# RWKV's sample group: four pairs of heads together in the odd mixer's second part, in place of one pair at a time

## The chip, the cores and the metric

The kernel runs on one core of one Trainium2 chip. The metric is the device time of one execution in microseconds (us); a comparison uses the median of several executions of each kernel.

## The reference, cut to what matters

One inference step of a two-layer decoder for a prompt (512 positions) and a group of 8 samples of 4 positions that share all weights, 544 columns in all. Each layer is FFN, mixer, FFN. The odd layer's mixer projects its input once, runs a dilated windowed attention (8 heads) and an RWKV-7 recurrence (8 heads of 64) beside each other, and joins them in one output projection. The change concerns the recurrence of the 8 samples, which start from given states:

```
def step(s, inp):
    r_t, w_t, k_t, v_t, kk_t, a_t = inp
    sk = jnp.einsum('bhvk,bhk->bhv', s, kk_t)
    s = (s * w_t[:, :, None, :] - sk[..., None] * (kk_t * a_t)[:, :, None, :]
         + v_t[..., None] * k_t[:, :, None, :])
    return s, jnp.einsum('bhvk,bhk->bhv', s, r_t)
...
s_final, ys = lax.scan(step, s0.astype(f32), seq)
```

Outputs are the mixed result of all 544 columns and the final states of the samples (8 x 8 heads of 64 x 64) and of the prompt.

## The kernel before, in words

The kernel is written with tiles: each tile has a name, a pool and a number of buffers, and a planner that runs when the program is built simulates the engines and fixes the order of the instructions on each of them. Among instructions that it holds ready, the one that stands earlier in the program goes first; a tile of a pool with one buffer can be written again only when all readers of the one before are through. Every engine then works through its own list in order; a DMA is issued by the engine whose queue it is given to (SP for nearly all loads, ACT or POOL for some) and waits there for its buffer.

`odd_mix` (line 1670) does the odd mixer. It has two parts with different PSUM banks (a PSUM bank holds 128 x 512 floats; there are eight).

The first part has the kinds mm 2, ps 2, rs 2, rx 1, ro 1. RWKV's 8 heads are worked as four pairs p = 0 to 3; two pairs make a group. For each pair:

- `rw_first(p)` (line 1336 on) is a generator in three pieces: projections and decays; the chunks' products (line 1422) and a round trip through DRAM (rab, rEA); and then the forward substitution of 31 steps of two short VectorE operations each (lines 1440 and 1441), its table's way through DRAM (rtb, and line 1445 back into the tile TT), MT (line 1449), RR (line 1448), KB, VU and QB. Most of its tiles have one buffer, so a pair's later pieces wait for the pair before.
- `odd_qk(h)` (line 1129 on), the attention's query and key projections, is put between to fill TensorE.
- `rw_inverse(p)` (line 1482 on) is some 300 small products in banks of the kind rs (lines 1498, 1514, 1519, 1523, 1528); its last evictions are on line 1531.
- `rw_rec(g)` (line 1533) is the recurrence over 16 chunks for a group: 15 steps of a small product (line 1544) and a VectorE addition (line 1545), then the output products (line 1552) and `rw_out`. The group's tiles MT, W, RR and Y have one buffer, so pair 2's MT and RR wait for the recurrence of group 0.
- `rw_sample(p)` (line 1585) is the sample group of one pair. It loads the pair's states (S0, 128 x 512, on ACT's queue, line 1597), and then goes through a chain: products of the small vectors held in SM (lines 1605 to 1608), a masked copy, products (1615, 1616), a few sums, products (1622), products (1626, 1627), the product with the state (1633), a masked product and a sum over it on VectorE (1635, 1636), small additions (1638), the products for the output (1641), a masked product on GpSimd (1644), the update product (1647), decay of the state on GpSimd (1648), their sum (1649) and the store (1650). Its small matrices lie in the tile rsw, its masked products in rum; rS0, rsw and rum have one buffer each. The trace drops digits from names (rS is rS0).

In the program's order pair 0 has: pieces of rw_first, odd_qk(0), rw_inverse(0), rw_sample(0); pair 1 the same with rw_rec(0) ahead of rw_sample(1); pair 2 rw_inverse(2) and rw_sample(2); pair 3 odd_qk(2) and rw_inverse(3).

The second part has the kinds mm 1, sc 4, sm 1, rx 1, ro 1. It holds rw_rec(1), rw_sample(3) in banks of the kind sm, odd_qk(3), then 16 attention units `odd_head(hp, i)` (line 1141 on), each of which copies its queries on GpSimd into qz (line 1155), uses two banks sc for the scores (1156), two for the transposed weights (1169) and one for the values (1178), with adaLN's products (line 185) between the last eight units, and then `odd_sample` (line 1191), the attention of the sample group. `odd_sample` goes through `sample_attn` (line 500) twice, for four samples each: scores (516), softmax, transposes (539 to 541), values (549), output (561). Its cache tiles (4 x 256 KB a sample) are loaded on line 1204 into a ring of five places: the two halves of rKB, the two halves of rVU, and rGP0. `rw_sample_end` (line 1652) finishes the samples' output, and the output projection follows, whose first product is line 460 with the tile mm.

What the change touches in `odd_mix`, all of it:

```
                if p < 3:
                    self.rw_sample(p)
...
            self.psum(mm=1, sc=4, sm=1, rx=1, ro=1)
...
            self.rw_rec(1, r0, a2)
            self.rw_sample(3, "sm")
            for h in (3,):
                self.odd_qk(h, a1)
```

Of the kernel before, what the change touches and what calls it, by code (L numbers as in the profile page):

```python
# [9 lines left out]
F32 = mybir.dt.float32  # L10
# [16 lines left out]
class Kern:  # L27
# [1557 lines left out]
    def rw_sample(self, p, kind="rs"):  # L1585
# [4 lines left out]
        SM, DC = self.SM[:, p], self.DC  # L1590
# [4 lines left out]
        E = lambda n: self.rsm.tile([128, 512], F32, name=n)  # L1595
        S0 = E("rS0")
        nc.scalar.dma_start(bv(S0), D["rw_s0"][:, p])
        w = E("rsw")

        MS = w[:, 0:96].rearrange("p (a t) -> p a t", a=3)  # L1600
        EV, T, BK, QT, UV, W = [w[:, i:j] for i, j in ((96, 192), (192, 224), (224, 288), (288, 352), (352, 416), (416, 480))]
        pa = bank()
        pv = pa[:, 0:96].rearrange("p (a t) -> p a t", a=3)
        for o, r0, r1 in heads:
            PE.matmul(pv[o, 0], SM[o, 0:2], SM[o, 6])
            PE.matmul(pv[o, 1:3], SM[o, 6:8], SM[o, 0:4:3])
            PE.matmul(pa[o, 128:192], SM[o, 4:6], self.ident[o, o])
            PE.matmul(pa[o, 192:256], SM[o, 0:2], self.ident[o, o])
        V.tensor_tensor(MS, pv, self.rc["rsmask"][:, 0:3], op=M)
        S_.activation(UV, pa[:, 192:256], AF.Copy, scale=self.rc["rbmt"][:, 8:9])  # L1610
        S_.activation(w[:, 224:352], pa[:, 128:256], AF.Copy)

        pa = bank()
        for o, r0, r1 in heads:
            PE.matmul(pa[o, 0:32], MS[o, 0:2], MS[o, 1])
            PE.matmul(pa[o, 32:96], MS[o, 1:3], UV[o])
        S_.activation(EV, pa[:, 0:96], AF.Copy)
        V.tensor_tensor(T, self.rc["rsmask"][:, 3], MS[:, 1], op=S)
        V.tensor_tensor(T, T, EV[:, 0:32], op=A)
        pa = bank()  # L1620
        for o, r0, r1 in heads:
            PE.matmul(pa[o, 0:32], MS[r0, 0:2], EV[r0, 0:32])
        V.tensor_tensor(T, T, pa[:, 0:32], op=S)
        px = bank()
        for o, r0, r1 in heads:
            PE.matmul(px[o, 0:32], QT[r0], T[r0])
            PE.matmul(px[r0, 32:96], T[r0], EV[r0, 32:96])
        S_.activation(SM[:, 2], px[:, 0:32], AF.Copy)
        for o, r0, r1 in heads:
            V.tensor_copy(UV[r0], px[r0, 32:96])  # L1630
        pa = bank()
        for o, r0, r1 in heads:
            PE.matmul(pa[o], SM[o, 2:4], S0[o])
        um = bv(E("rum"))
        V.tensor_tensor(um, bv(pa), b8, op=M)
        V.tensor_reduce(W, um.rearrange("p b v -> p v b"), axis=AX.X, op=A)
        for o, r0, r1 in heads:
            V.tensor_tensor(UV[r0], UV[r0], W[r0], op=A)
        pa = bank()
        for o, r0, r1 in heads:  # L1640
            PE.matmul(pa[o, 0:64], MS[o, 1:3], UV[o])
        V.tensor_tensor(self.ys[:, p], W, pa[:, 0:64], op=A)

        G.tensor_tensor(um, UV.unsqueeze(1).to_broadcast([128, 8, 64]), b8, op=M)
        pa = bank()
        for o, r0, r1 in heads:
            PE.matmul(pa[o], BK[o], um[o].rearrange("p b v -> p (b v)"))
        G.tensor_tensor(bv(S0), bv(S0), DC[:, p, 16:24].unsqueeze(2).to_broadcast([128, 8, 64]), op=M)
        V.tensor_tensor(S0, S0, pa, op=A)
        nc.sync.dma_start(D["d_wkv_s"][:, p], bv(S0))  # L1650

# [18 lines left out]
    def odd_mix(self):  # L1670
# [6 lines left out]
        with es:  # L1677
# [29 lines left out]
            for p in range(4):  # L1707
# [10 lines left out]
                if p < 3:  # L1718
                    self.rw_sample(p)
# [300 lines left out]
```

## Time and profile before

| what | value |
|---|---|
| three executions | 2569.62, 2573.84, 2588.95 us; median 2573.84 |
| the profiled execution | 2567.64 us; its span, first to last instruction, 2565.8 us |
| mean granted TensorE clock | 0.969 of full speed |
| TensorE busy | 2442.6 us, 95% of the span |
| VectorE, ScalarE, GpSimd busy | 1232.4, 943.3 and 409.0 us |
| the odd mixer's steps spoken of here | some 1790 to 2078 us of the span |

PE is TensorE's matmul, PEld its weight load (beside it), DVE VectorE, ACT ScalarE, POOL GpSimd, SP SyncE; a q behind an engine's name is its queue of issues. Times are us from the span's start. A matmul's end is modelled, so that of two that follow each other closely the records overlap. The granted clock is a share of full speed: 1.00 is 2.4 GHz, 0.50 is 1.2 GHz.

### The profile page before, as it was taken

The numbers are of one execution on the slowest core, as the hardware profiler recorded it, in microseconds if no ns is written. First come the engines' busy times: TensorE is split into PE (matmuls) and PEld (weight loads), VectorE is DVE, ScalarE is ACT, GpSimd is POOL, SyncE is SP. The second block draws the span as 40 slices with busy tenths as digits, with TensorE's granted clock in tenths as the row PEclk, the third lists the DMA queues.
The fourth block names the chain that finished last, engine by engine and source line by source line (L and its number), as shares of the span: only waits on it lengthen the run. The fifth ranks groups of instructions, "written<-read, shape, count | busy, mean of one in ns | idle before, by whom it ended". The sixth has DMA issues, their size and how long they took to land.

```text
span 2565.8 us, 50682 instructions
## 1 busy us (share of the span) xinstructions
PE 2442.6 (95%) x20338; PEld 2253.4 (88%) x20338; DVE 1232.4 (48%) x2999; ACT 943.3 (37%) x2051; POOL 409.0 (16%) x616
## 2 busy tenths in 40 slices
PE   6999999899899999999999999889999999999996
PEld 4988999897588999999989999878877578999996
DVE  6532356544577333345423334558664567333343
ACT  4322323435555333224323322545422545333222
POOL 1000016411432000031000003312111122000032
PEclk8999999999999999999999999889988999999998
DMA  7666335567632222223562232322322632222221
GB/s 237 203 217 216 113 118 112 188 216 252 222 122 75 87 88 94 80 80 105 173 222 83 85 91 81 103 77 78 92 75 92 211 113 74 87 89 94 80 80 58
DMA packets 184027, 318.27 MB, mean 124 GB/s; under 512 B 38416, under 2 KB 47040, under 8 KB 183664
## 3 DMA queue, kind: packets, MB, share of 16 engines
q1 hardware_dynamic: 172096, 282.52, 34.6%
q0 software_dynamic: 10400, 31.06, 4.1%
q8 instruction: 159, 2.61, 0.4%
q10 hardware_dynamic: 1296, 1.46, 0.2%
q14 instruction: 76, 0.62, 0.1%
HBM read 288.68 MB, written 26.28 MB: 123 GB/s over the span
## 4 chain that ended last, share of the span: by engine, by line
PE 82%; DVE 7%; DMA 4%; ACT 4%; issue 1%; POOL 1%; SPq 1%; ACTq 0%; POOLq 0%; DVEq 0%
PE mm L460 23%; PE mm L462 23%; PE mm L461 22%; PE ps L185 2%; DVE x L347 1%; DMA ar<-in_ada_w 1%; DMA raw<-in_ada_w 1%; ACT t L249 1%; DVE wl L449 1%; PE sc L1178 1%; PE sc L1156 1%; PE ad L185 1%; PE ps L460 1%; PE ps L462 1%; PE ps L461 1%
## 5 line engine op out<-in xcount | busy, mean ns | idle before, releaser
L460 PE MATMUL mm<-xh,wh 128*128 128x272 f32 x3720 | 1089.4, 295 | 35.5 <-ACT xh L250 10.1
L461 PE MATMUL mm<-xl,wh 128*128 128x272 f32 x3720 | 1082.7, 291 | 2.0 <-DVE xl L251 2.0
L462 PE MATMUL mm<-xh,wl 128*128 128x272 f32 x3720 | 1083.0, 292 | 0.8 <-DVE wl L449 0.8
L460 PEld LDWEIGHTS mm<-xh,wh 128*128 128x128 f32 x3720 | 706.0, 190 | 85.2 <-ACT t L401 31.2
L449 DVE TENSOR_TENSOR wl<-raw,wh 128x512 fp32r<-128x512 f32 (+1 forms) x664 | 458.8, 703 | 537.0 <-ACT wh L448 505.0
L461 PEld LDWEIGHTS mm<-xl,wh 128*128 128x128 f32 x3720 | 710.5, 191 | 7.0 <-DVE xl L251 2.5
L462 PEld LDWEIGHTS mm<-xh,wl 128*128 128x128 f32 x3720 | 706.6, 190 | 7.8 <-issue 4.2
L448 ACT ACTIVATE wh<-raw 128x512 fp32r<-128x512 f32 (+1 forms) x664 | 401.5, 618 | 727.6 <-PE mm L461 565.9
L460 PE MATMUL mm<-hh,wh 128*128 128x272 f32 x1280 | 370.4, 289 | 0.0
L462 PE MATMUL mm<-hh,wl 128*128 128x272 f32 x1280 | 370.4, 289 | 0.0
L461 PE MATMUL mm<-hl,wh 128*128 128x272 f32 x1280 | 369.5, 289 | 0.0
L460 PEld LDWEIGHTS mm<-hh,wh 128*128 128x128 f32 x1280 | 241.4, 189 | 0.8 <-issue 0.4
L461 PEld LDWEIGHTS mm<-hl,wh 128*128 128x128 f32 x1280 | 241.2, 188 | 0.4
L462 PEld LDWEIGHTS mm<-hh,wl 128*128 128x128 f32 x1280 | 241.1, 188 | 0.4
L402 DVE TENSOR_TENSOR t<-t,mm 128x272 f32<-128x272 f32 x169 | 73.4, 434 | 279.6 <-ACT t L401 279.4
L401 ACT ACTIVATE t<-mm 128x272 f32<-128x272 f32 x169 | 65.6, 388 | 318.6 <-PE mm L462 318.6
L297 POOL TENSOR_TENSOR sa<-x 128x272 f32<-128x272 f32 x24 | 26.1, 1087 | 907.4 <-DVE x L291 852.0
L291 DVE SCALAR_TENSOR_TENSOR x<-mm,rg,x 128x272 f32<-128x272 f32 (+1 forms) x96 | 45.9, 479 | 171.4 <-PE mm L462 170.7
L466 DVE TENSOR_TENSOR hl<-t,hh 128x272 fp32r<-128x272 f32 x160 | 69.6, 439 | 35.8 <-ACT hh L465 35.3
L465 ACT ACTIVATE hh<-t 128x272 fp32r<-128x272 f32 x160 | 67.5, 426 | 38.5 <-DVE t L402 38.5
L277 POOL TENSOR_TENSOR sq<-sq,t 128x272 f32<-128x272 f32 x60 | 54.7, 926 | 18.1 <-ACT t L276 17.3
L249 ACT ACTIVATE t<-x,S,G 128x272 f32<-128x272 f32 (+1 forms) x80 | 44.5, 589 | 24.1 <-DVE x L348 23.5
(643 smaller groups left out, 2536.6 us busy)
## 6 DMA issues: line engine op xcount, KB each, us to landing
raw<-in_ada_w SPq DMA_DIRECT2D x192, 256.0 KB
raw<-in_wg SPq DMA_DIRECT2D x176, 256.0 KB
raw<-in_wu SPq DMA_DIRECT2D x176, 256.0 KB
raw<-in_wd SPq DMA_DIRECT2D x160, 256.0 KB
ar<-in_ada_w SPq DMA_DIRECT2D x96, 256.0 KB
raw<-in_odd_rw SPq DMA_DIRECT2D x28, 256.0 KB
xs<-x POOLq DMA_DIRECT2D x16, 272.0 KB, 4.0
x<-xs POOLq DMA_DIRECT2D x8, 544.0 KB, 7.8
```

What stands on the lines that cost most here:

```text
L185: return nc.tensor.matmul(ps[32 * j:32 * j + 32], self.c32[:, 9 * k:9 * k + 32], r, start=(k == 0), stop=(k == 7))
L249: nc.scalar.activation(t[:, 0:n], x[:, d, c0:pe], AF.Identity, scale=G[:, d, 0:1], bias=S[:, d, 0:1])
L277: G.tensor_tensor(s["q"], s["q"], t, op=A)
L401: self.act = nc.scalar.activation(s, pss[2 * i], AF.Silu)
L402: mul = nc.vector.tensor_tensor(s, s, pss[2 * i + 1], op=ALU.mult)
L448: nc.scalar.activation(wh[:, 0:w], r[:, 0:w], AF.Copy)
L449: (lo or nc.vector).tensor_tensor(wl[:, 0:w], r[:, 0:w], wh[:, 0:w].bitcast(F32), op=ALU.subtract)
L460: nc.tensor.matmul(ps, wh[:, s], mh, start=first, stop=False)
L461: nc.tensor.matmul(ps, wh[:, s], ml, start=False, stop=False)
L462: self.last = nc.tensor.matmul(ps, wl[:, s], mh, start=False, stop=last)
L465: self.nc.scalar.activation(hi, src, AF.Copy)
L466: return (lo_eng or self.nc.vector).tensor_tensor(lo, src, hi.bitcast(F32), op=ALU.subtract)
```

## The change

`rw_sample` now takes all four pairs. It stands once, in the second part, behind rw_rec(1); the calls for pairs 0 to 2 in the first part are gone. The front of the chain (to the copies into UV) is done for all four pairs phase by phase: the eight heads' products of a phase go into one bank (two in the first phase), and the small VectorE and ACT operations take two pairs each. The small matrices lie in the tiles rKB (pairs 0 and 1) and rVU (pairs 2 and 3) in place of rsw. Then a loop over the pairs does the rest (the state product on, lines 1633 to 1650 of before), with the same operations as before, S0 in two buffers and rum in one. S0 is loaded on GpSimd's queue in place of ACT's. The second part's banks are mm 1, sc 3, sm 2, rx 1, ro 1.

```diff
--- before.py
+++ after.py
@@ -1582,72 +1582,83 @@
         else:
             nc.sync.dma_start(self.rob[:, :, c], o)
 
-    def rw_sample(self, p, kind="rs"):
+    def rw_sample(self, pool, kind):
 
         nc, D = self.nc, self.D
         V, G, S_, PE = nc.vector, nc.gpsimd, nc.scalar, nc.tensor
         M, A, S = ALU.mult, ALU.add, ALU.subtract
-        SM, DC = self.SM[:, p], self.DC
         bank = lambda: self.bank[kind].tile([128, 512], F32, name=kind)
         bv = lambda t: t.rearrange("p (b v) -> p b v", b=8)
         b8 = self.rc["rbmt"][:, 0:8].unsqueeze(2).to_broadcast([128, 8, 64])
         heads = [(slice(64 * h, 64 * h + 64), slice(64 * h, 64 * h + 32), slice(64 * h + 32, 64 * h + 64)) for h in range(2)]
-        E = lambda n: self.rsm.tile([128, 512], F32, name=n)
-        S0 = E("rS0")
-        nc.scalar.dma_start(bv(S0), D["rw_s0"][:, p])
-        w = E("rsw")
-
...
+        each = [(p, *h) for p in range(4) for h in heads]
+        SM, mask = self.SM, self.rc["rsmask"]
+
+        ws = [self.rg.tile([128, 2, 512], F32, name=n) for n in ("rKB", "rVU")]
+        cut = lambda i, j: [w[:, :, i:j] for w in ws]
+        one = lambda v: [v[p // 2][:, p % 2] for p in range(4)]
+        MS2, EV2, T2, BQ2, UV2 = cut(0, 96), cut(96, 192), cut(192, 224), cut(224, 352), cut(352, 416)
+        MS = [m.rearrange("p (a t) -> p a t", a=3) for m in one(MS2)]
+        EV, T, BQ, UV, W = [one(v) for v in (EV2, T2, BQ2, UV2, cut(416, 480))]
+        quad = lambda t, n: [t[:, 2 * n * i:2 * n * i + 2 * n].rearrange("p (a n) -> p a n", a=2) for i in range(2)]
+        of = lambda v, p: v[p // 2][:, p % 2]
+        pa, pb = quad(bank(), 96), quad(bank(), 128)
+        for p, o, r0, r1 in each:
+            sm = SM[:, p]
+            m = of(pa, p).rearrange("p (a t) -> p a t", a=3)
+            PE.matmul(m[o, 0], sm[o, 0:2], sm[o, 6])
+            PE.matmul(m[o, 1:3], sm[o, 6:8], sm[o, 0:4:3])
+            PE.matmul(of(pb, p)[o, 0:64], sm[o, 4:6], self.ident[o, o])
+            PE.matmul(of(pb, p)[o, 64:128], sm[o, 0:2], self.ident[o, o])
+        for i in range(2):
+            V.tensor_tensor(MS2[i], pa[i], mask[:, 0:3].rearrange("p a t -> p (a t)").unsqueeze(1).to_broadcast([128, 2, 96]), op=M)
+            S_.activation(UV2[i], pb[i][:, :, 64:128], AF.Copy, scale=self.rc["rbmt"][:, 8:9])
+            S_.activation(BQ2[i], pb[i], AF.Copy)
+
+        pa = quad(bank(), 96)
+        for p, o, r0, r1 in each:
+            PE.matmul(of(pa, p)[o, 0:32], MS[p][o, 0:2], MS[p][o, 1])
+            PE.matmul(of(pa, p)[o, 32:96], MS[p][o, 1:3], UV[p][o])
+        for i in range(2):
+            S_.activation(EV2[i], pa[i], AF.Copy)
+            V.tensor_tensor(T2[i], mask[:, 3].unsqueeze(1).to_broadcast([128, 2, 32]), MS2[i][:, :, 32:64], op=S)
+            V.tensor_tensor(T2[i], T2[i], EV2[i][:, :, 0:32], op=A)
+        pa = quad(bank(), 32)
+        for p, o, r0, r1 in each:
+            PE.matmul(of(pa, p)[o], MS[p][r0, 0:2], EV[p][r0, 0:32])
+        for i in range(2):
+            V.tensor_tensor(T2[i], T2[i], pa[i], op=S)
+        px = quad(bank(), 96)
+        for p, o, r0, r1 in each:
+            PE.matmul(of(px, p)[o, 0:32], BQ[p][r0, 64:128], T[p][r0])
+            PE.matmul(of(px, p)[r0, 32:96], T[p][r0], EV[p][r0, 32:96])
+        for i in range(2):
+            S_.activation(SM[:, 2 * i:2 * i + 2, 2], px[i][:, :, 0:32], AF.Copy)
+            for o, r0, r1 in heads:
+                V.tensor_copy(UV2[i][r0], px[i][r0, :, 32:96])
+        for p in range(4):
+            S0 = pool.tile([128, 512], F32, name=f"rS0{p % 2}")
+            nc.gpsimd.dma_start(bv(S0), D["rw_s0"][:, p])
+            pa = bank()
+            for o, r0, r1 in heads:
+                PE.matmul(pa[o], SM[o, p, 2:4], S0[o])
+            um = bv(pool.tile([128, 512], F32, name="rum"))
+            V.tensor_tensor(um, bv(pa), b8, op=M)
+            V.tensor_reduce(W[p], um.rearrange("p b v -> p v b"), axis=AX.X, op=A)
+            for o, r0, r1 in heads:
+                V.tensor_tensor(UV[p][r0], UV[p][r0], W[p][r0], op=A)
+            pa = bank()
+            for o, r0, r1 in heads:
+                PE.matmul(pa[o, 0:64], MS[p][o, 1:3], UV[p][o])
+            V.tensor_tensor(self.ys[:, p], W[p], pa[:, 0:64], op=A)
+
+            G.tensor_tensor(um, UV[p].unsqueeze(1).to_broadcast([128, 8, 64]), b8, op=M)
+            pa = bank()
+            for o, r0, r1 in heads:
+                PE.matmul(pa[o], BQ[p][o, 0:64], um[o].rearrange("p b v -> p (b v)"))
+            G.tensor_tensor(bv(S0), bv(S0), self.DC[:, p, 16:24].unsqueeze(2).to_broadcast([128, 8, 64]), op=M)
+            V.tensor_tensor(S0, S0, pa, op=A)
+            nc.sync.dma_start(D["d_wkv_s"][:, p], bv(S0))
 
     def rw_sample_end(self):
         nc, rw = self.nc, self.rw
@@ -1715,11 +1726,9 @@
                 self.rw_inverse(p, *self.f[p])
                 if p == 1:
                     self.rw_rec(0, r0, p2)
-                if p < 3:
-                    self.rw_sample(p)
             nc.sync.dma_start(D["d_shift"], self.dsh)
             ea.close()
-            self.psum(mm=1, sc=4, sm=1, rx=1, ro=1)
+            self.psum(mm=1, sc=3, sm=2, rx=1, ro=1)
             a1, pE, a2 = pool("oa3", 1), pool("rre", 2), pool("oa2", 2)
             for n, d in (("dmask", "dmask"), ("mold", "dmold"), ("smask", "dmnew")):
                 setattr(self, n, self._ld(a1, d))
@@ -1732,7 +1741,7 @@
             self.aoT = a1.tile([128, 4, SP], F32, name="aoT")
             self.ro1 = a1.tile([128, 2, SP], F32, name="ro1")
             self.rw_rec(1, r0, a2)
-            self.rw_sample(3, "sm")
+            self.rw_sample(self.rsm, "sm")
             for h in (3,):
                 self.odd_qk(h, a1)
```

## Rows read from the trace of the kernel before

**Rows 1.** The page: busy time by engine (first line), chain that ended last

```profile
PE 2442.6 (95%) x20338; PEld 2253.4 (88%) x20338; DVE 1232.4 (48%) x2999; ACT 943.3 (37%) x2051; POOL 409.0 (16%) x616
...
PE 82%; DVE 7%; DMA 4%; ACT 4%; issue 1%; POOL 1%; SPq 1%; ACTq 0%; POOLq 0%; DVEq 0%
```

**Rows 2.** Busy time by stretch: length, engines, granted clock, DMA share, GB/s

```profile
1790.00:1830.00 40.00, 38.95 (x491) 33.49 (x489) 29.98 (x100) 17.33 (x40) 6.17 (x16) 1.00 0.36 101
1830.00:1880.00 50.00, 49.00 (x774) 41.66 (x774) 24.64 (x63) 16.52 (x36) 6.16 (x15) 0.97 0.23 68
1880.00:1904.00 24.00, 19.02 (x339) 16.70 (x339) 17.84 (x37) 4.22 (x11) 9.54 (x11) 0.57 0.18 45
1904.00:1935.00 31.00, 27.12 (x268) 23.10 (x268) 22.48 (x89) 9.82 (x23) 6.86 (x15) 0.98 0.50 151
1935.00:1956.00 21.00, 20.98 (x349) 19.34 (x349) 6.07 (x16) 3.88 (x9) 0.11 (x1) 0.55 0.12 40
1956.00:2078.00 122.00, 115.52 (x890) 68.23 (x887) 64.58 (x223) 58.87 (x164) 13.99 (x36) 0.97 0.47 154
```

**Rows 3.** PE's waits, 1956 to 2078 us: total, times, longest

```profile
PE sc L1169 <- DVE aP L1163: 3.5, 1, 3.5
PE mm L185 <- DMA ar<-in_ada_w: 1.5, 1, 1.5
PE sc L1178 <- ACT wT L1171: 1.3, 2, 1.0
```

**Rows 4.** Timeline: start, length, engine, line, instruction [idle before it, and its releaser]

```profile
1795.83 0.39 SPq L1445 DMA_DIRECT2D rTT<-rtb  x1
...
1813.06 0.68 DVE L1649 TENSOR_TENSOR rS<-rS,rs 128x512 f32<-128x512 f32 x1
...
1814.67 1.59 PE L1498 MATMUL rs<-rQB,rTT 32*64 32x128 f32 x32
```

**Rows 5.** Timeline of GpSimd: the first MT of the second group

```profile
1880.13 3.76 POOL L1449 TENSOR_TENSOR rMT<-rid,rDC 128x1024 f32<-128x1024 f32 x2 [14.13 <-PE rx L1544]
```

**Rows 6.** Busy time beside the four pairs' sample groups: tile rsw, then rSM

```profile
sum 106.00, PE 12.93 PEld 6.43 DVE 11.97 ACT 2.89 POOL 4.67; mean PE 3.23 PEld 1.61 DVE 2.99 ACT 0.72 POOL 1.17
...
sum 106.00, PE 8.87 PEld 4.52 DVE 0.00 ACT 0.79 POOL 1.34; mean PE 2.22 PEld 1.13 DVE 0.00 ACT 0.20 POOL 0.33
```

**Rows 7.** Timeline of the second part: last inverse, pair 3, attention's samples, output projection

```profile
1955.72 0.59 ACT L1531 ACTIVATE rY<-rs 64x512 f32<-64x512 f32 x1 [3.63 <-PE rs L1528]
...
1958.05 0.30 PE L1605 MATMUL sm<-rSM 64*64 64x32 f32 x2
...
1973.99 1.08 PE L1633 MATMUL sm<-rS,rSM 64*64 64x512 f32 x4
...
1975.12 0.69 DVE L1635 TENSOR_TENSOR rum<-sm,c_rbmt 128x512 f32<-128x512 f32 x1 [0.87 <-PE sm L1633]
...
1981.88 1.07 PE L1647 MATMUL sm<-rum,rsw 64*64 64x512 f32 x4
...
1986.73 0.40 PE L516 MATMUL sm<-rVU,sq 128*32 128x256 f32 x1
...
2078.34 0.37 PE L460 MATMUL mm<-xh,wh 128*128 128x272 f32 x1
```

**Rows 8.** Timeline: substitution of pair 3 (first, last), copies inside it, its inverse

```profile
1906.14 0.19 DVE L1440 TENSOR_TENSOR rtm<-rU,rEA 128x31 f32<-128x31 f32 x1
...
1923.45 0.45 DVE L1630 COPY rsw<-rs 32x64 f32<-32x64 f32 x2 [0.58 <-ACT rSM L1628]
...
1927.06 0.18 DVE L1441 TENSOR_TENSOR rU<-rU,rtm 128x8 f32<-128x8 f32 x1
...
1934.89 5.80 PE L1498 MATMUL rs<-rQB,rTT 32*64 32x128 f32 x64 [3.07 <-DMA rTT<-rtb]
```

**Rows 9.** POOL's DMA queue: issues with size and time to landing; one issue

```profile
xs<-x POOLq DMA_DIRECT2D x16, 272.0 KB, 4.0
...
1930.63 0.58 POOL L1229 DMA_DIRECT2D c_dmask<-in_dmask  x1
```

More of the change, by code (lines that the diff above doesn't have):

```diff
@@ L1594, in rw_sample @@
         heads = [(slice(64 * h, 64 * h + 64), slice(64 * h, 64 * h + 32), slice(64 * h + 32, 64 * h + 64)) for h in range(2)]
-        E = lambda n: self.rsm.tile([128, 512], F32, name=n)
-        S0 = E("rS0")
-        nc.scalar.dma_start(bv(S0), D["rw_s0"][:, p])
-        w = E("rsw")
[L1600 to L1648, printed above, removed]
@@ L1649, in rw_sample @@
-        V.tensor_tensor(S0, S0, pa, op=A)
-        nc.sync.dma_start(D["d_wkv_s"][:, p], bv(S0))
+        each = [(p, *h) for p in range(4) for h in heads]
[4 more added lines that the diff above has]
+        MS2, EV2, T2, BQ2, UV2 = cut(0, 96), cut(96, 192), cut(192, 224), cut(224, 352), cut(352, 416)
```

## The prediction, made before the change was run

> **What bounds the kernel now.** I read the page first: TensorE (PE) is busy 95% of the span and holds 82% of the chain that ended last [rows 1]. A mean over the span says nothing of the mixer that is changed, so the second view is busy time by stretches of the odd mixer, cut where its steps change [rows 2]. In it PE is busy 38.95 of 40 us and 49.00 of 50 us up to 1880 us; 19.02 of 24 us at a granted clock of 0.57, where VectorE (DVE) has 17.84; 27.12 of 31 us; 20.98 of 21 us at a clock of 0.55 (much of it at the lower level, 1.2 GHz); and 115.52 of 122 us in the mixer's second part. So both the place that loses work and the place that gains it are held by PE, and between them lie stretches held by a chain of dependences. The third view, who waited for whom, says how much room PE has in the second part: three groups of waits, 3.5 + 1.5 + 1.3 = 6.3 us [rows 3].
>
> The chain in the first part is read from the timeline. Two facts carry it. One: rw_inverse of pair 1 needs the PSUM banks "rs", of which there are two, and the sample group of pair 0 has them. The table TT of pair 1 was requested at 1795.83; pair 0's last use of a bank is the DVE addition at 1813.06, and the inverse's first product starts at 1814.67, right behind it [rows 4]. Two: the MT buffer of pair 2 is free when the recurrence rw_rec of group 0 is through: GpSimd waited 14.13 us for a product of line 1544, until 1880.13 [rows 5]. All of pair 2's and pair 3's later steps stand behind that point.
>
> **The change, part by part.** *PE work that moves.* The number of products is the same; the pairs only share banks. One pair's products are busy in the rows of the tiles rsw and rSM: (12.93 + 8.87) / 4 = 5.45 us [rows 6]; this counts overlapping tails, so three pairs are at most 16.3 us. They leave the first part and enter the second.
>
> *First part, pairs 0 and 1.* They lie in the stretches where PE is nearly full, so up to 2 x 5.45 = 10.9 us comes off the way to the point at 1880. It can be less, down to 0: the planner fills the gaps between the steps of the recurrence with other products that are ready, and what takes the place of the sample products stretches the steps again. It can be more: the banks are free, so the inverse of pair 1 need no longer wait from the landing of TT (an estimate: 1795.83 plus the 3.07 us that PE waited for the same load of pair 3 [rows 8], so about 1799) to 1814.67, some 15 us; PE is full meanwhile, so this pays only as far as other products can move behind 1880, where PE has 5 us idle in 24 [rows 2]. I take 11, near the busy rows, and keep 0 and 22 as ends.
>
> *First part, pair 2.* It runs beside the forward substitution of pair 3, 62 short DVE operations from 1906.14 to 1927.06, after which TT goes out and back and PE starts at 1934.89 after 3.07 us of waiting [rows 8]. PE is not the bound there; DVE is. Of the sample group the mask product, two small sums, a difference and two copies lie in between, about 1.25 us, of which the copies' 0.45 has a row, and before those DVE waited 0.58 us for ScalarE (ACT) [rows 8]: 1.8 us comes off, at least 0. What is late next is PE itself: without pair 2's products it idles about 5.45 - 1.8 = 3.6 us longer before 1934.89, and that costs nothing more, since the stretch behind it already runs at 0.55 [rows 2].
>
> So the start of the last inverse comes 11 + 1.8 = 12.8 us earlier.
>
> *Second part: PE.* Here 16.3 us are added to a stage with 6.3 us of waits [rows 3]. The waits lie behind ACT, DVE and a weight load late in the stage, while the sample products come early; they can't all fill them. Ends: +16.3 with nothing absorbed, +10.0 with all. I take about half, 3, absorbed: +13.3.
>
> *Second part: the other engines.* DVE gets 11.97 / 4 = 2.99 us a pair from the tile rsw [rows 6] and two passes of 0.69 (one of them is in [rows 7]), 4.4 in all, 13 for three pairs, less by the joined small operations (each now does two pairs). DVE has 64.58 busy of 122 [rows 2], so this lies beside PE: 0. If that cover were gone it would be up to 13. ACT's share is 2.89 / 4 = 0.7 a pair: 0.
>
> *Second part: the sample chain and what waits for it.* The four pairs' small matrices now live in rKB and rVU, which are also the ring into which the dilated attention's sample group loads its cache. Before, that ring was free when the last inverse ended (its last eviction is at 1955.72), and the first score product came at 1986.73, after pair 3's group had given back the one "sm" bank [rows 7]. Now the ring is free only after all four pairs. For one pair the front (products at 1958.05 up to the state product at 1973.99) took 16 us, and a loop from the masked product at 1975.12 to the end of the update product at 1981.88 + 1.07 took 7.8 us [rows 7]. The buffer rum is single, so the loops follow each other: 16 + 4 for the larger front (three more pairs at some 3 us of PE each, more than half of it inside the gaps) + 4 x 7.8 = 51 us, plus 2.3 before it starts and about 5 until two cache tiles have landed: the first score comes 59 us behind 1955.72, against 31. Then the sample group of the attention has to end with the rest: it took from 1986.73 to 2078.34, 91.6 us, interleaved with the attention units, which go ahead of it. With 13.3 us more the stage lasts 122.6 + 13.3 = 136 and leaves it 136 - 59 = 77. If it can't be shortened the stage is 59 + 91.6 = 150.6 long, 14.7 more. Much of the 91.6 is waiting in PE's order behind units, and these will be further on by then; I take +2, ends 0 and +15. The cache loads stand in SP's queue, and behind them the adaLN weights and the output projection's first strips wait if the planner puts the loads too early; that is inside the same ends.
>
> *PSUM banks.* The units' "sc" banks go from four to three; each of 16 units takes five. The nearest price is a product that waits for ACT to evict: 1.3 us for two [rows 3], 0.65 each, so up to 10 if every unit waits once more. "sm" gets a second bank, which the attention's sample group uses eight times: up to -5. I take 0 for both together.
>
> *The state loads* go from ACT's queue to GpSimd's (POOL). The nearest rows: an issue of the same size took POOL 0.58 us, and a POOL-queue transfer of 272 KB landed after 4.0 us [rows 9]. The first two have free buffers and can go early; those of pairs 2 and 3 wait until the state two pairs back has been stored, and behind the waiting issue on POOL stand the pairs' own products and the copies of queries (qz) for the units' scores. Ends 0 and 2 x 4.0 = 8; I take 0, because a whole loop of 7.8 us lies between, and if that cover is gone it is the 8. The Trainium skill ("SBUF — State Buffer", in "SBUF: two separate sides") speaks against this edit: a DMA issued from GpSimd has its descriptors written there, and certain VectorE instructions lock GpSimd out meanwhile, so it advises the ACT or SP queue. No row here shows such a stall; by that rule the sum would be longer by a DVE pass or two, some 2 us.
>
> **Sum.** -11 - 1.8 + 13.3 + 2 = +2.5. The profiled execution took 2567.6 us (span 2565.8), so 2570.1; the median of the three runs, 2573.84, lies 6.2 above the profiled one, so the median to be expected is 2576.
>
> **Rivals.**
> 1. *The freed banks decide.* The inverse of pair 1 starts about 15 us earlier and the recurrence of group 0 follows, so the first part gains the 22 instead of 11, while the second part pays its 13.3 + 2. For it: the inverse starts 0.9 us after the last read of the bank. Against it: PE has nothing free before 1880. -22 - 1.8 + 15.3 = -8.5: 2565.
> 2. *The attention's sample group becomes the tail* (the other side: slower). It begins 28 us later and keeps its 91.6 us, so PE runs dry at the end of the mixer and the output projection waits. For it: its steps (scores, softmax, values, output, twice over) are a chain, its 8 MB come through a ring of five tiles, and the ring is held until the last pair. Against it: PE was full nearly all that time, so part of the 91.6 is queueing. It decides as soon as the first score comes later than 136 - 91.6 = 44 us behind the last inverse without the chain getting shorter. -12.8 + 28 = +15.2: 2589; with no gain from pairs 0 and 1 it is -1.8 + 28 = +26.2: 2600.
> 3. *A mere move.* The first part's gaps are filled by other products (0 in place of -11), the second absorbs all 6.3: -1.8 + 10 + 2 = +10: 2584.
>
> **How the numbers follow.** Forecast (both parts nearly cancel) 0.45; rival 1 0.2; rival 2 0.2; rival 3 0.15. The range takes the first part at its best with all waits absorbed (-23.8 + 10 = -13.8, 2560) to rival 2 with no gain from pairs 0 and 1 and a little of the lost "sc" bank: 2560 to 2602. One per cent, 26 us, is what a measurement of this kernel can surely tell. Only rival 2's worse half goes beyond it on the slow side (above 2599.6): 0.11. For faster than 2548 the second part would have to take the added 16 us for nothing and the first give 22: 0.06. The rest, 0.83, is within.
>
> **What would show it.** In the changed profile: PE's waits in the second part stay at a few us and that part, from the last eviction of the last inverse to the first output projection, is 136 us long, not 122.6; the last inverse begins near 1922 instead of 1934.89; GpSimd's wait at line 1449 ends near 1869; the first score of the attention's sample group comes some 59 us behind the last inverse. Rival 1 shows as an inverse of pair 1 near 1800 and the point at 1880 moved to below 1862; rival 2 as PE idle in the last 20 us of the mixer beside products of the sample attention; rival 3 as a point at 1880 that has not moved. The forecast is wrong if the second part grows by less than 8 or more than 24 us, or if time changes outside the odd mixer.

## The result, and the profile after

The changed kernel takes 2598.16 us, the kernel before 2581.52 us (medians of 13 executions each, on the same chip): ratio 1.0064, 95% interval 1.0048 to 1.008, some 16.5 us slower. The forecast was +2.5 us. That the time moves by less than one per cent was right; that the two parts nearly cancel was not: by the trace the first part gives 5.6 us and the second takes 19.8. The profiled execution has a span of 2596.4 us. The page, busy time and the chain that ended last:

```profile
PE 2460.0 (95%) x20338; PEld 2263.6 (87%) x20338; DVE 1232.7 (47%) x2987; ACT 945.4 (36%) x2045; POOL 409.2 (16%) x620
...
PE 84%; DVE 6%; DMA 4%; ACT 3%; issue 2%; SPq 1%; POOL 1%; another core or an unknown queue 0%; ACTq 0%; DVEq 0%; POOLq 0%
```

The number of products is that of before, and the shares are nearly so [rows 1]: the page alone tells next to nothing. Places in the mixer are compared from one anchor, the last GpSimd addition of line 347 ahead of the mixer, at 1634.18 us before and 1649.02 us after. (The 14.84 us between the two are not the change's doing, so they do not break the forecast's condition that nothing changes outside the mixer. Up to the anchor both traces have the same work, 12310 and 12313 products, with PE busy 1575.4 and 1590.1 us at a granted clock of 0.99 and 0.98; and over the traces of all the experiments the anchor lies anywhere from 1634.65 to 1652.54 us, with the old sample group and with the new one.) The same stretches as in [rows 2], columns as there, and the waits of PE in the second part (line, releaser, total, times, longest):

```profile
1803.60:1843.60 40.00, 36.14 (x432) 32.50 (x431) 24.44 (x79) 15.38 (x32) 3.75 (x12) 0.87 0.33 87
1843.60:1890.00 46.40, 45.81 (x805) 40.20 (x803) 22.85 (x62) 16.78 (x36) 6.26 (x16) 1.00 0.22 62
1890.00:1913.40 23.40, 18.25 (x282) 16.09 (x275) 16.91 (x35) 4.41 (x12) 8.23 (x11) 0.56 0.20 56
1913.40:1944.10 30.70, 21.52 (x217) 19.65 (x215) 18.66 (x77) 8.82 (x19) 5.13 (x13) 0.93 0.45 136
1944.10:1965.40 21.30, 21.28 (x350) 19.65 (x351) 6.07 (x16) 3.90 (x9) 0.00 (x0) 0.54 0.01 2
1965.40:2107.50 142.10, 131.98 (x1035) 77.24 (x1034) 76.24 (x248) 64.94 (x179) 21.40 (x44) 0.96 0.44 146
```

```profile
PE sc L1169 <- DVE aP L1163: 2.4, 2, 1.3
PE sc L1178 <- ACT wT L1171: 2.2, 5, 0.7
PE sm L549 <- DMA rGP<-in_ccv: 1.8, 1, 1.8
PE sm L516 <- DMA rVU<-in_cck: 1.5, 1, 1.5
```

Two things are to be seen. The first part now has idle PE where it was full (36.14 of 40 us, against 38.95 of 40) and much more in front of the last inverse (21.52 of 30.7, against 27.12 of 31). The second part has 16.5 us more PE work (131.98 against 115.52) and did not lose its idle time: 10.1 us against 6.5. Over the whole way from the anchor to the output projection, before and then after:

```profile
1634.20:2078.30 444.10, 406.98 (x4438) 329.15 (x4436) 270.62 (x798) 191.62 (x448) 81.84 (x184) 0.91 0.34 106
```

```profile
1649.00:2107.50 458.50, 408.87 (x4435) 329.34 (x4434) 269.88 (x787) 194.87 (x450) 83.96 (x186) 0.90 0.33 102
```

PE's busy time grew by 1.9 us and the way by 14.4: the change moves work, and what it loses is idle time of PE (37.1 us before, 49.6 after). Up to the last eviction of the last inverse PE has some 14 us less of busy time, and the way is only 5.5 us shorter; behind it PE has some 16 us more, and the way is 19.8 us longer.

The places by which the steps were to be judged, from the timeline. Lines moved: 1633 of before is 1644, 1647 is 1658.

```profile
1822.90 1.36 PE L1498 MATMUL rs<-rQB,rTT 32*64 32x128 f32 x27
1888.69 3.76 POOL L1449 TENSOR_TENSOR rMT<-rid,rDC 128x1024 f32<-128x1024 f32 x2 [17.90 <-PE rx L1544]
1944.09 5.80 PE L1498 MATMUL rs<-rQB,rTT 32*64 32x128 f32 x64 [7.39 <-DMA rTT<-rtb]
1965.10 0.59 ACT L1531 ACTIVATE rY<-rs 64x512 f32<-64x512 f32 x1 [3.80 <-PE rs L1528]
1991.21 1.08 PE L1644 MATMUL sm<-rS,rSM 64*64 64x512 f32 x4
2025.90 1.08 PE L1658 MATMUL sm<-rum,rVU 64*64 64x512 f32 x4
2032.82 0.40 PE L516 MATMUL sm<-rVU,sq 128*32 128x256 f32 x1
2095.54 0.60 PE L561 MATMUL sm<-c_cst,sO 128*128 128x128 f32 x4
2107.52 0.57 PE L460 MATMUL mm<-xh,wh 128*128 128x272 f32 x1
```

| from the anchor, or as named | before | after | forecast |
|---|---|---|---|
| first product of the inverse of pair 1 | 180.5 | 173.9 | (rival 1: some 15 earlier) |
| GpSimd's MT of pair 2 (line 1449) | 246.0 | 239.7 | 235 |
| first product of the last inverse | 300.7 | 295.1 | 287.9 |
| last eviction of it to first attention score | 31.0 | 67.7 | 59 |
| last eviction of it to first output projection | 122.6 | 142.4 | 136 |

So the first part gives 5.6 us instead of 12.8, and the second takes 19.8 instead of 13.3 + 2: +14.2 by the two traces, beside +16.5 by the timed executions. The last product of the attention's sample group (line 561) lies 12 us ahead of the end: it is not the tail that rival 2 expected.

### The profile page after: what moved, and what is told of

Its sections match the earlier page's. It is cut to its first block, busy times and chain, and to the rows that moved or that the text cites. A ratio compares the mean times of both kernels' runs of the same rounds, so it can differ in the third digit from the quotient of the medians.

```text
span 2596.4 us, 50666 instructions
## 1 busy us (share of the span) xinstructions
PE 2460.0 (95%) x20338; PEld 2263.6 (87%) x20338; DVE 1232.7 (47%) x2987; ACT 945.4 (36%) x2045; POOL 409.2 (16%) x620
## 4 chain that ended last, share of the span: by engine, by line
PE 84%; DVE 6%; DMA 4%; ACT 3%; issue 2%; SPq 1%; POOL 1%; another core or an unknown queue 0%; ACTq 0%; DVEq 0%; POOLq 0%
PE mm L460 23%; PE mm L462 23%; PE mm L461 23%; PE ps L185 2%; DVE x L347 1%; DVE wl L449 1%; PE sc L1156 1%; PE sc L1178 1%; ACT t L249 1%; PE ad L185 1%; PE sc L660 1%; DMA ar<-in_ada_w 1%; PE ps L460 1%; PE rs L1498 1%; PE ps L462 1%
## 5 line engine op out<-in xcount | busy, mean ns | idle before, releaser
L291 DVE SCALAR_TENSOR_TENSOR x<-mm,rg,x 128x272 f32<-128x272 f32 (+1 forms) x96 | 45.9, 479 | 173.1 <-PE mm L462 172.5
L249 ACT ACTIVATE t<-x,S,G 128x272 f32<-128x272 f32 (+1 forms) x80 | 44.5, 589 | 23.9 <-DVE x L348 23.2
```

What stands on the lines that cost most here:

```text
L249: nc.scalar.activation(t[:, 0:n], x[:, d, c0:pe], AF.Identity, scale=G[:, d, 0:1], bias=S[:, d, 0:1])
```

## The experiments

Each was timed beside the kernel before on the same chip; ratios are to it, with their 95% intervals. "The mixer's start" in the expectations is the anchor above.

**1. The three pairs left out** (their outputs and states are missing; ys is set to zero once).

```diff
-                if p < 3:
-                    self.rw_sample(p)
```

> The kernel before without the sample groups of pairs 0 to 2 (left out altogether: their outputs and states are missing). It prices what their absence gives in the first part alone. Theory (what the changed kernel's trace shows: the last inverse 6.3 us earlier): ratio to before 0.9975, about -6 us, last inverse some 6 us earlier in the odd mixer. By the prediction's terms (11 + 1.8): 0.995, -12.8 us. If a mere move: 0.9993, at most -1.8 us. Second part unchanged, 122 to 123 us, by all three.

Measured: 0.9981 (0.9972 to 0.999), some 5 us less (3 to 7 by the interval). Last inverse at 295.4 us from the anchor, second part 121.9 us. The absence is worth 5 us, not 12.8: the same 5 that the changed kernel's first part shows (its last inverse is at 295.1), so the absence of the groups accounts for what that part does. Whether the freed banks or the work that is gone did it, this run doesn't part.

**2. The same, with 14 us of loose products in the second part** (the three pairs left out here too).

```diff
             self.rw_sample(3, "sm")
+            for _ in range(3):
+                ps = self.sc()
+                for _ in range(5):
+                    for o in (0, 64):
+                        nc.tensor.matmul(ps[o:o + 64], self.SM[o:o + 64, 3, 0:2], self.dmask[o:o + 64])
```

> The kernel before without the sample groups of pairs 0 to 2 (left out: their outputs and states), and in the second part, behind pair 3's group, 30 products of 64x512 on constants that nobody reads, some 16 us of TensorE work in three sc banks: the work of the three pairs with none of their chain. Theory (in the second part TensorE's work decides; the chain adds little): 13 to 16 us over the kernel without the three pairs, which stood at 0.9981, so ratio to before 1.003 to 1.0045. Rival (the chain of the four pairs is what costs, loose work would be absorbed): at most 6 us over it, ratio 0.998 to 1.0005.

Measured: 1.0031 (1.0015 to 1.0046), 12.8 us above experiment 1 (0.0050 x 2570). The products, from the groups of the second part (times, busy us, mean ns, idle before), and then the stretch from the last eviction to the output projection, with the columns of [rows 2]:

```profile
L1739 PE MATMUL sc<-c_dmask,rSM 64*64 64x512 f32 x60 | 14.3, 592 | 0.0
```

```profile
1970.70:2106.70 136.00, 127.21 (x959) 72.74 (x958) 65.76 (x224) 62.80 (x175) 13.06 (x36) 0.99 0.42 139
```

14.3 us of products that wait for no other engine, and that take from the units only a bank of the kind sc three times, make the part 14.1 us longer (136.0 against 121.9). In length nothing is absorbed: PE's busy time is 10.8 us more (127.21 against 116.40, at a granted clock of 0.99 against 0.97) and its idle time 3.3 more (8.8 against 5.5). So the growth of idle time in the changed kernel does not need the sample chain: more work early in the part alone brings it. What is left between this kernel and the changed one (142.4 - 136.0 = 6.4 us) is mostly busy time too (131.98 - 127.21 = 4.8), at a granted clock of 0.96 there against 0.99 here; it is not parted further.

**3. Moved, but not joined.**

```diff
-            self.rw_sample(3, "sm")
+            for p in range(4):
+                self.rw_sample(p, "sm")
```

(and the calls of the first part gone, as in 1).

> The kernel before with the calls for pairs 0 to 2 moved, one pair at a time, in front of pair 3's in the second part: nothing batched, four sc banks, one sm bank, states on ACT's queue, the ring not held by small matrices. Theory (the added TensorE work of 16 us in a full part decides, the way it is grouped does not): ratio 1.006 to 1.008, +16 to +20 us, as the changed kernel. Rival (the length of the sample chain decides): four chains of 16 + 7.8 us one behind the other are 95 us, the one sm bank is held until then, the attention's sample group starts about 100 us behind the last inverse and ends late: ratio 1.015 to 1.02.

Measured: 1.0173 (1.0156 to 1.0191), +44.5 us: the rival. From its timeline, the four masked products, the first score and the last product of the attention's samples, and then the last 20 us up to that product:

```profile
1970.17 0.69 DVE L1635 TENSOR_TENSOR rum<-sm,c_rbmt 128x512 f32<-128x512 f32 x1 [0.87 <-PE sm L1633]
1995.98 0.69 DVE L1635 TENSOR_TENSOR rum<-sm,c_rbmt 128x512 f32<-128x512 f32 x1 [0.87 <-PE sm L1633]
2025.54 0.69 DVE L1635 TENSOR_TENSOR rum<-sm,c_rbmt 128x512 f32<-128x512 f32 x1
2055.81 0.69 DVE L1635 TENSOR_TENSOR rum<-sm,c_rbmt 128x512 f32<-128x512 f32 x1
2063.06 0.63 PE L516 MATMUL sm<-rVU,sq 128*32 128x256 f32 x1 [0.84 <-DVE rS L1649]
...
2123.30 0.66 PE L561 MATMUL sm<-c_cst,sO 128*128 128x128 f32 x4 [0.79 <-DVE sO L558]
```

```profile
2104.00:2124.00 20.00, 15.07 (x65) 6.39 (x61) 4.30 (x10) 1.66 (x4) 1.88 (x4) 0.70 0.38 123
```

A pair takes 26 to 30 us, the first score comes 112.3 us behind the last inverse's last eviction (1950.78), and the attention's sample group ends at 172.5, with PE idle for 4.9 of the last 20 us. Here rival 2 of the prediction is what happens. The changed kernel's form (joined, two banks, and the small things that come with them) is thus worth 28 us (1.0173 - 1.0064) against the plain move: the theory that only the work counts falls for this kernel. It fits the changed one, where the chain ends 12 us ahead of the units.

**4. The banks of before under the changed kernel.**

```diff
-            self.psum(mm=1, sc=3, sm=2, rx=1, ro=1)
+            self.psum(mm=1, sc=4, sm=1, rx=1, ro=1)
```

> The changed kernel with the banks of before in the second part (sc 4, sm 1 in place of sc 3, sm 2). Theory (the split of the banks is worth nothing): ratio to before 1.0064 within 0.0015. Rival a (the fourth sc bank is missed by the units, 4 to 10 us): 1.0025 to 1.005. Rival b (the second sm bank carries the sample chain): slower, 1.008 or more.

Measured: 1.0102 (1.0087 to 1.0117): rival b. The second "sm" bank is worth some 10 us, net of the "sc" bank that it costs (0.0038 x 2570; the interval ends allow 2 to 18). In its trace a pair's loop, from one state product to the next, takes 11.7 to 12.9 us, against 8.3 to 10.0 in the changed kernel; the first score comes 80.5 us behind the last eviction (2035.22 - 1954.77), the last product of the attention's samples at 149.6, behind the last unit (129.4): they are the tail again.

```profile
1954.77 0.59 ACT L1531 ACTIVATE rY<-rs 64x512 f32<-64x512 f32 x1 [3.87 <-PE rs L1528]
2035.22 0.40 PE L516 MATMUL sm<-rVU,sq 128*32 128x256 f32 x1
2104.35 0.66 PE L561 MATMUL sm<-c_cst,sO 128*128 128x128 f32 x4 [0.79 <-DVE sO L558]
```

**5. The ring freed earlier.**

```diff
-        ring = [KB[:, 0], KB[:, 1], VU[:, 0], VU[:, 1], self.rg.tile([128, 512], F32, name="rGP0")]
+        ring = [self.rg.tile([128, 512], F32, name=f"rGP{i}") for i in range(2)] + [KB[:, 0], KB[:, 1], VU[:, 0], VU[:, 1]]
...
-            t = [ring[(slot + i) % 5] for i in range(2)]
+            t = [ring[(slot + i) % 6] for i in range(2)]
```

> The changed kernel with the cache ring of the attention's sample group in six places, rGP0 and rGP1 first, then the halves of rKB and rVU: the first four cache tiles then wait only for pairs 0 and 1, not for all four pairs. Theory (TensorE's work decides): the first score comes up to 20 us earlier, TensorE's waits for cache tiles (1.8 + 1.5 + 0.6 = 3.9 us) go at most, ratio to before 1.005 to 1.0064. Rival (the late start of the attention's sample group decides): the second part is 10 to 20 us shorter, ratio 0.999 to 1.0025.

Measured: 1.0074 (1.0061 to 1.0086), not told apart from the changed kernel. The rival falls (the second part is 145.4 us long, not shorter), but the theory's detail was wrong as well: the first score came 3 us earlier, not 20.

```profile
2003.23 0.46 SPq L1204 DMA_DIRECT2D rKB<-in_cck  x1
2021.04 1.26 PE L1658 MATMUL sm<-rum,rVU 64*64 64x512 f32 x4
2022.40 0.69 DVE L1660 TENSOR_TENSOR rS<-rS,sm 128x512 f32<-128x512 f32 x1
2023.28 0.64 PE L516 MATMUL sm<-rKB,sq 128*32 128x256 f32 x1
```

The tiles of the first score were asked for at 2003, and it started at 2023.28: 0.2 us behind the VectorE sum that reads the last pair's update product out of its bank (line 1660). In the changed kernel the last two tiles were asked for only at 2027.05, right behind that product, and the score came at 2032.82. So here the ring no longer holds it; it starts as something would that waits for the pairs' "sm" banks, which stand earlier in the program (no run tests this by itself; experiment 4 has the price of the second bank). PE's waits for the first cache tiles were gone; a wait of 4.6 us at line 1169 stood in their place.

**6. The state loads on ACT's queue.** In the loop, `nc.gpsimd.dma_start` becomes `nc.scalar.dma_start`.

> The changed kernel with the state loads on ACT's queue, as before. Theory (the queue is worth nothing, since the loads have a whole loop of time): the changed kernel's own ratio, 1.0064 to 1.0075. Rival (GpSimd's queue delays them or is stalled by VectorE): 2 us or more faster, ratio 1.0055 or less. Other side (an issue on ACT waits there for the store of the state two pairs back, and ACT's evictions behind it): 1.009 or more.

Measured: 1.0047 (1.0029 to 1.0065), against the changed kernel's 1.0064 (1.0048 to 1.008): the middle lies in the rival's range, the intervals overlap, and this stays open. In the trace the second part is 146.4 us long, not shorter than the changed kernel's 142.4. The Trainium skill ("SBUF — State Buffer", "SBUF: two separate sides") advises the ACT or SP queue; no run here shows a price for GpSimd's that can be told from none.

**7. The groups kept in the first part, in banks of the kind ps.**

```diff
-                    self.rw_sample(p)
+                    self.rw_sample(p, "ps")
```

> The kernel before with the sample groups of pairs 0 to 2 where they were, but in banks of the kind ps in place of rs: the inverse of pair 1 no longer waits for a bank, while the TensorE work stays in the first part. It parts the 5 us that the absent groups gave. If they came from the freed banks: the inverse of pair 1 starts 174 us behind the mixer's start (180.5 before), the point of line 1449 near 240 (246 before), ratio 0.998. If from the TensorE work that was gone: the point stays at 245 to 247 although the inverse starts early, ratio 0.9995 to 1.0005. The three groups of ps against the transposes and projections that use ps: up to 1.003.

Measured: 1.0099 (1.0083 to 1.0115), +25 us: none of the three. The inverse of pair 1 starts 196.8 us from the anchor, 16.3 later than before. Projections, head sums and transposes all use the two ps banks, and the next pair's tiles come out of these. Pair 1's first transpose (line 1333) comes 171.2 us from the anchor, against 143.0 before: the chain held in ps set back the steps that feed the next pair by 28 us. This does not part the 5 us between freed banks and absent work.

**8 and 9. The groups late in the first part**, behind the inverse of pair 2, in rs (8) or ps (9).

```diff
-                if p < 3:
-                    self.rw_sample(p)
+                if p == 2:
+                    for q in range(3):
+                        self.rw_sample(q)
```

> The kernel before with the calls for pairs 0, 1 and 2, one pair at a time in rs banks, all behind the inverse of pair 2 (in the first part). Theory (between the point where MT of pair 2 comes free and the last inverse TensorE has some 14 us of idle time when no sample group lies before it, and the chain there is VectorE's): the first part keeps the 5 us of the absent groups, the last inverse begins 295 to 300 us behind the mixer's start (300.7 before), ratio 0.9975 to 0.9995. Rival (three chains in the rs banks and their VectorE operations delay the substitution of pair 3 and its inverse): last inverse later than 301, ratio 1.001 to 1.006.

> The same with the three groups in banks of the kind ps, so that no inverse waits for a bank that they hold. Theory: last inverse 295 to 300 us behind the mixer's start, ratio 0.9975 to 0.9995, no worse than with rs banks. Rival (VectorE and the transposes of pair 3, which use ps, are delayed): ratio 1.001 to 1.006.

Measured: 1.0089 (1.0073 to 1.0104) and 1.0074 (1.0055 to 1.0094): the rivals. The point of line 1449 came at 240.9 in both, 5 us early, as without the groups; the last inverse at 324.6 and 325.6, 24 us late. Experiment 8, the request of its table, the third group's masked product and the inverse:

```profile
1949.04 0.38 SPq L1445 DMA_DIRECT2D rTT<-rtb  x1
1970.54 0.69 DVE L1635 TENSOR_TENSOR rum<-rs,c_rbmt 128x512 f32<-128x512 f32 x1 [1.94 <-PE rs L1633]
1975.91 0.47 PE L1498 MATMUL rs<-rQB,rTT 32*64 32x128 f32 x2
```

The table was asked for at 1949, and the inverse stood 27 us behind it until the third group had its rs banks through. PE was busy 15.18 of these 26.9 us. In experiment 9 the groups held no rs bank, but pair 3's transposes, which need ps, came right behind the third group's update product, and the inverse behind them at 1978.08:

```profile
1967.74 1.97 PE L1647 MATMUL ps<-rum,rsw 64*64 64x512 f32 x4 [0.71 <-POOL rum L1644]
1969.64 0.69 PE L1333 MATMUL ps<-c_cst,rQR 128*128 128x128 f32 x2
```

In both, idle time of PE was no use to work that holds a bank which the next step needs.

**10 to 12. Work that fills the first part's gaps**, to see whether a version beats both. The changed kernel no longer uses the pool rsm in the first part; opened in the second, it leaves room there for the heads 6 and 7's queries and keys.

```diff
-            self.rsm = pool("rsm", 1)
...
-                for h in ((0,), (1,), (), (2,))[p]:
+                for h in ((0,), (1,), (), (2, 3))[p]:
...
+            self.rsm = pool("rsm", 1)
...
-            for h in (3,):
-                self.odd_qk(h, a1)
```

(10; in 11 odd_qk(3) stands behind the last inverse, in 12 the list is `((0,), (1,), (2,), (3,))`.)

> The changed kernel with the query and key projections of the last heads (odd_qk(3)) taken out of the second part and put behind odd_qk(2), ahead of the last inverse; the pool of the sample group's states, which the change no longer uses in the first part, is opened in the second, which makes the room. Theory (the first part has some 14 us of idle TensorE between the point of line 1449 and the last inverse, the second part is TensorE's): the second part gives back what these projections take, the first grows by less: ratio 0.999 to 1.003. Rival (the projections stretch the chain to the last inverse as the late sample groups did): 1.005 to 1.009.

> The same, with odd_qk(3) behind the last inverse in the program's order, so that it only fills gaps there and the rest of it comes after. Theory: ratio 0.999 to 1.003, the last inverse as early as in the changed kernel (295 us behind the mixer's start). Rival (it runs wholly after the inverse, since nothing of it is ready before or no bank is free): 1.005 to 1.007, as the changed kernel.

> As the one before the last, but with odd_qk(2) ahead of the inverse of pair 2 and odd_qk(3) ahead of that of pair 3. Theory: what the stretches behind the point of line 1449 can't hide is then ahead of it, where TensorE is full: between 0.999 and 1.005, no better than with both ahead of the last inverse.

Measured: 1.0058 (1.0045 to 1.0071), 1.0034 (1.0021 to 1.0047) and 1.0129 (1.011 to 1.0147). Only 11 gains on the changed kernel, by 0.0030, some 8 us, and still loses 9 to the kernel before. Number 10 is where its rival had it, 11 lies between its theory and its rival, and 12 was no better than 10, as expected, but by more than its range. Stretches of 11 (from 23 us behind the point of line 1449 on), then PE's waits for adaLN's weights in 12:

```profile
1895.30:1929.30 34.00, 31.23 (x274) 29.54 (x273) 19.16 (x77) 10.35 (x22) 2.13 (x6) 0.90 0.46 139
1929.30:1954.50 25.20, 19.61 (x366) 14.40 (x367) 7.12 (x18) 3.73 (x9) 4.42 (x11) 0.73 0.43 139
1954.50:2086.30 131.80, 121.49 (x961) 67.12 (x960) 75.00 (x244) 62.10 (x167) 20.06 (x42) 0.95 0.41 132
```

```profile
PE mm L185 <- DMA ar<-in_ada_w: 21.3, 7, 6.0
```

The second part is 10.6 us shorter than the changed kernel's (131.8 against 142.4; 10.5 us less busy), and the first pays 1.9 for it (last eviction at 318.0 from the anchor, 316.1 there): work that holds no bank of the chain does fill those gaps. It is not odd_qk(3) alone: 24 of adaLN's 64 products (line 185; 4.9 us) came ahead into the last inverse as well, where the changed kernel has none. That has a price that no expectation counted, a wait of PE for their weights: 0.6 us in the changed kernel, 4.9 in 11, 6.5 in 10 and 21.3 in 12. No version found here beats the kernel before.

## Why the prediction was right or wrong, step by step

The measured time lies in the range that was given, and the second part pays for the work as forecast; but the two parts do not cancel. The range reached that far up because of rival 2, whose tail did not come, so that the result fell inside is in part luck. The steps, one by one:

**First part, pairs 0 and 1: -11 forecast, -6.3 measured** (246.0 to 239.7). The step "up to 2 x 5.45 = 10.9 us comes off, I take 11, near the busy rows" failed by size. From the last eviction of the first inverse to the point of line 1449, before and after, with PE's longest wait there after:

```profile
1788.60:1880.10 91.50, 89.44 (x1300) 76.56 (x1295) 55.90 (x168) 34.95 (x77) 12.33 (x31) 0.98 0.28 81
```

```profile
1802.20:1888.70 86.50, 82.21 (x1204) 73.08 (x1198) 47.69 (x144) 33.26 (x69) 8.71 (x28) 0.94 0.27 74
```

```profile
PE rs L1498 <- DVE rVU L1501: 3.9, 1, 3.9
```

96 products are gone, two pairs of 48. Of their 10.9 us busy time fell by only 7.2, at a granted clock of 0.94 against 0.98 (0.87 in 1803.6 to 1843.6), and idle time grew by 2.2. So about half of the work taken away did come off (the stretch is 5.0 us shorter; the other 1.3 us lie ahead of it), a part went into idle time, and the rest, an estimate by difference, into products at the lower clock. The idle time is mostly one wait of 3.9 us: the inverse of pair 1, which now comes early, waits for a VectorE operation of its own and PE has nothing else ready; before, the longest wait there was 1.6 us. A stretch that is 97% full loses work only as far as the work left is ready to close the gap. The prediction named this ("down to 0") and took nothing off for it. Rival 1 was right that the inverse of pair 1 comes early (by 6.6 us, not 15), and wrong that this decides.

**Pair 2: -1.8 forecast, +0.6 measured** (the start of the last inverse behind that point: 54.8 to 55.4). The substitution did get shorter, by 1.5 us (from 21.1 us [rows 8] to 19.6), but it began 1.1 us later behind the point (26.0 to 27.1), after a wait for its table from DRAM:

```profile
1915.75 0.19 DVE L1440 TENSOR_TENSOR rtm<-rU,rEA 128x31 f32<-128x31 f32 x1 [1.19 <-DMA rEA<-rab]
1935.20 0.18 DVE L1441 TENSOR_TENSOR rU<-rU,rtm 128x8 f32<-128x8 f32 x1
```

What the step also forgot was the table's way through DRAM behind it. Issue by issue on SP, before and after:

```profile
1927.65 2.57 SPq L1444 DMA_DIRECT2D rtb<-rU  x4
1931.61 0.38 SPq L1445 DMA_DIRECT2D rTT<-rtb  x1
```

```profile
1931.09 1.88 SPq L202 DMA_DIRECT2D ar<-in_ada_w  x4
1934.02 0.37 SPq L446 DMA_DIRECT2D raw<-in_odd_out  x1
1935.40 2.65 SPq L1444 DMA_DIRECT2D rtb<-rU  x4
1941.56 0.38 SPq L1445 DMA_DIRECT2D rTT<-rtb  x1
```

From writing the table to asking for it back went 4.0 us before and 6.2 after. Just ahead of it now come loads of the second part (adaLN and projection weights on SP, masks on GpSimd's queue at 1934.00; before, the masks came behind the write, and no adaLN weights stood near it). Experiment 1's trace has the same order, and 6.5 us. That the loads are the cause is read from this order and the row below; no run tests it. The DMA engines' busy tenths after, 40 slices of 1934 to 1945 us:

```profile
DMA  9987989899999999999999960000000499100000
```

They are full until about 1940.5 and idle when the table is asked for; PE waits 7.39 us in all. A part is won back behind the request: from the last step of the substitution to the inverse it is 8.7 us, against 7.7. So +1.1 - 1.5 + 1.1 is the +0.6. That the longer wait costs nothing more (as forecast) is right for PE's clock: 0.54 against 0.55 in the inverse.

**Second part, the work: 16.3 us forecast, 16.5 measured**, right. "The second absorbs 3 of the 6.3 us of waits": wrong; it absorbed nothing. Experiment 2 shows it with loose products, 14.3 us for 14.1. The old waits shrank (3.5 us at line 1169 to 2.4), and others took their place.

**The chain: +2 forecast.** Its working was near: the front 23.3 us from the first product (1967.88) to the state product against 20, four loops of about 9 us against 7.8, the first score at 67.7 against 59. And the conclusion held: the attention's sample group was shortened from 90.6 us (31.0 to 121.6) to 62.7 (67.7 to 130.4) and ended ahead of the units. Most of the shortening does not need the second "sm" bank: with one (experiment 4) the group takes 69.1 us. What was missed is what the second bank adds: with one, the group starts 12.8 us later and ends last.

**The banks: 0 forecast for both together.** Wrong: the split is worth about 10 us to the changed kernel. The prediction's ends for the two (up to 10 lost, up to 5 won) had the second bank too cheap: it priced the eight uses by the attention's sample group and left out the pairs' own 17 (five in the front, three in each loop), where the loops of 11.7 to 12.9 us in place of 8.3 to 10.0 show the gain.

**GpSimd's queue: 0 forecast**; not contradicted, not settled (experiment 6).

The sum: -6.3 + 0.6 in the first part, +0.2 in the last inverse itself, +16.5 of work and 3.3 of more idle time in the second = +14.3 in place of +2.5. Among the rivals the second had the nearest number (+15.2) by a mechanism that did not occur. The third, a mere move at +10, is nearest in kind: part of the first part's gain vanishes into gaps. But the second part absorbs none of the cost.

## What to carry to other kernels

Here, moving work out of a stage that was full gained less than the work, and putting it into a full stage cost all of it: price the two ends differently, the first by what else is ready there, the second at one for one. Count idle time as well as work: the busy time of PE in the mixer hardly changed, and the loss was idle time left behind. A short chain is judged by what it holds, not by the time of its engines: the same products, one pair at a time in PSUM banks that others wait for, cost 19 to 45 us in the four other places tried, and joining the steps, with a second bank, was worth 28 us. When the order of the work changes, look at which loads now stand ahead of a small one that a chain waits for: the request for a table of 128 KB came 2.2 us later behind its write.

## What the runs showed that was not expected

A small table's write and the request to read it back lay 2.2 us further apart with other loads ahead of them; over its whole way that was 1.1 us, which with a start 1.1 us later ate the 1.5 us that VectorE had saved. The last inverse ran at a granted clock of 0.55 before and 0.54 after, though PE had been busy 27.12 of 31 us in front of it in one and 21.52 of 30.7 in the other; behind 31.23 busy of 34 us, in experiment 11, the stretch of the inverse had 0.73.
